# Scan denominators, attention tiles, state residues, loads and an opening run of dense work, in a two-batch hybrid encoder layer

## The chip, the core and the metric

The kernel runs on one core of a Trainium2 chip. The metric is the device time of one execution in microseconds (us). The engines follow their own instruction streams: PE multiplies matrices, ACT (ScalarE), DVE (VectorE) and POOL (GpSimd) work element by element, and SP does nothing here but issue DMA transfers. An engine takes its instructions in order, and an instruction waits where what it needs isn't there, with all that is queued behind it on that engine.

## The reference, cut to what matters

One layer is applied to two batches with the same weights: A, the prompt (1024 tokens), and B, the sample (512 tokens).

```
h = rms_norm(x, pre_w);  cols = h @ w_in          # q|k, v, o, z, gates; attention q,k,v and z; merge gates
mLSTM, 4 heads x 256, both directions, in chunks of 128 tokens:
  sc  = (q k^T) * exp(d_log - mt)
  num = sc v + wa * (q C);   den = sum(sc) + wa * (q n)
  h   = num / max(|den|, exp(-mt))
  C   = decay * C + (k * ws)^T v                  # carried from chunk to chunk
  y_m = o * headnorm(h_fwd + h_bwd) * silu(z)
attention, 3 dilations x 8 heads x 64: logits, row max, exp, product with v, and per head
  y_a = (dilations weighted by their softmax denominators) * silu(z)
merged = sig(g0) * (y_m @ w_pm) + sig(g1) * (y_a @ w_pa)
y = x + rms_norm(merged @ w_out, post_w)
```

All is fp32. The kernel makes a fp32 product out of three matmuls of rounded halves (`mm3`, L194 to L196: high by high, high by low, low by high), so that every weight and activation first gets a high part (ACT, a copy) and a low part (the original less the high part, on DVE or POOL).

## The kernel before

**Two parts.** Up to 1056 us the wide input projections are made, by code that the change does not touch. From 1056 us on PE carries two kinds of work at once: the scans and attentions, whose steps depend on each other through ACT, DVE and POOL, and *dense* units (more columns of the input projection, then `w_pm`, `w_pa`, `w_out`), which depend only on their weights. The dense work is dealt out between the dependent steps so that PE has something to do while the other engines work. The stages, with the dense steps that `STEPS` gives them, are: the scan of A (210 steps, 1056 to 1345 us), the attention of A (202, to 1640 us), the scan of B with the combination of A's dilations beside it (164, to 1835 us), the attention of B (290, to 2100 us), and the combination of B and the last units (86 and what is left, to the end).

**Dense steps and weight tiles.** A dense step is three 128x512 matmuls. Eight steps use one weight tile of 128x1024: SP loads it into one of two buffers `wraw` (L210), ACT makes the high part `wh` (L252), DVE the low part `wl` (L253). There are three pairs of `wh` and `wl` in the scan of A. A `wraw` buffer is loaded anew only after its `wl` is made. `fill.stage(steps, shares)` sets the rate: in the scan of A there are `lead + 74 - 4` shares, `lead` of which are spent at once, ahead of the first product `a` of the scan; with `lead` 4 the rate is 210/74 = 2.84 steps a share and 11 steps go ahead.

**The scan of A** (`mlstm`) has 64 rounds: 4 heads, 8 chunks, 2 directions. `front(k)` makes the weights of a round: POOL masks a row of logarithms (`rm`, L924), ACT takes the exponential (L926), DVE multiplies (L927), ACT rounds (`sch`, L930), POOL takes the rest (`scl`, L931). `core(k)` multiplies: `num` (three or nine matmuls into a PSUM buffer, of which there are two), `kv` (the state's update). Then DVE updates the state `cf` (L977 or L980), ACT copies its high part `ch` (L983), DVE takes its low part `cl` (L984). The denominator follows: DVE takes the maximum (L987) and the reciprocal (L988). In the first half of a head's chunks ACT writes the quotient into `hacc` (L990; the profile calls its buffer X), in the second half DVE adds it there (L993). Only then is the PSUM buffer of `num` free for the round two later, so that PE's `num` waits for L990 or L993.

**The scan of B** (`mlstm_short`) has the same chain of maximum, reciprocal and quotient, at L1186 to L1191.

**The attentions** (`attend`, `att_round`) put a tile through four stages in successive rounds: products `lg` (PE, L1387), softmax (L1399 to L1404), transposes and eviction (`pt` L1410, `pts` L1413), and the product with v (`o` L1422, evicted to `ot` at L1424). There are 12 units u of 8 tiles (A) or 4 tiles (B). The loads of unit u+1 are put in a list when the second tile of unit u begins, and `spread(rounds)` deals them out to SP over so many rounds; the attention of B deals 12 loads over 3 rounds.

**The combination** (`combine`) loads three tiles for each block of 128 tokens (`og`), weighs and adds them. The load for block t+1 is issued when block t begins.

**What sets the order.** The orders of PE and SP are those of the code. For DVE, ACT and POOL a scheduler orders the instructions by priority (the place in the code, unless something is put ahead) and by its own estimate of when they can run. `tc.high_priority()` gives what stands in it a higher priority; `tc.issue_after(x)` keeps what stands in it behind instruction x.

Of the kernel before, what the change touches and what calls it, by code (L numbers as in the profile page):

```python
# [22 lines left out]
F32 = mybir.dt.float32  # L23
# [152 lines left out]
class Net:  # L176
# [680 lines left out]
    def mlstm(self, T, fill, steps, first, banks, lead, after, beside=()):  # L857
# [10 lines left out]
        with ExitStack() as stack:  # L868
# [80 lines left out]
            def core(k):  # L949
                h, i, d = rounds[k]  # L950
                x, m = head[h], made.pop(k)
                c = i if d == 0 else n - 1 - i
                cs = slice(c * P, (c + 1) * P)
                rw = m["rw"]
                v = (x["v"][0][:, c], x["v"][1][:, c])
                if i == d == 0:
                    self.need(("v", h))
                C = x["C"]
                pn = psum("num")
                self.mm3(pn[:, :258], m["sc"], v, True, i == 0)  # L960
                fill(1 / 3)
                if i < n - 1:
                    kh, kl = m["k"]
                    pc = psum("kv")
                    for ct in range(2):
                        self.mm3(pc[:, ct, :258], (kh[:, ct], kl[:, ct]), v, True, True)
                    fill(1 / 3)
                if i > 0:
                    qh, ql = m["q"]
                    _, ch, cl = C[d]  # L970
                    for ct in range(2):
                        self.mm3(pn[:, :258], (qh[:, ct], ql[:, ct]), (ch[:, ct], cl[:, ct]), False, ct == 1)
                if i < n - 1:
                    e = P - 1 if d == 0 else 0
                    if i == 0:
                        cf = sb.tile([P, 2, 258], F32, name=f"cf{d}", bufs=1)
                        nc.vector.tensor_copy(cf, pc[:, :, :258])  # L977
                    else:
                        cf = C[d][0]
                        nc.vector.scalar_tensor_tensor(cf, cf, rw[:, 1, e:e + 1], pc[:, :, :258], op0=OP.mult, op1=OP.add)  # L980
                    ch = sb.tile([P, 2, 258], F32R, name=f"ch{d}", bufs=1)
                    cl = sb.tile([P, 2, 258], F32R, name=f"cl{d}", bufs=1)
                    nc.scalar.activation(ch, cf, AF.Copy)  # L983
                    nc.vector.tensor_sub(cl, cf, ch.bitcast(F32))  # L984
                    C[d] = (cf, ch, cl)
                r = sb.tile([P, 4], F32, name="r", bufs=4)
                nc.vector.tensor_scalar(r[:, 1:2], pn[:, 256:257], m["fl"], pn[:, 257:258], op0=OP.max, op1=OP.max)  # L987
                nc.vector.reciprocal(r[:, 2:3], r[:, 1:2])  # L988
                if i < n // 2:
                    nc.scalar.activation(hacc[:, c], pn[:, :256], AF.Copy, scale=r[:, 2:3])  # L990
                    return
                hs = hacc[:, c]
                nc.vector.scalar_tensor_tensor(hs, pn[:, :256], r[:, 2:3], hs, op0=OP.mult, op1=OP.add)  # L993
                hn = hn_of()
                nc.scalar.activation(hn, hs, AF.Square, accum_out=r[:, 0:1])
                nc.gpsimd.tensor_scalar(r[:, 1:2], r[:, 0:1], 16.0 / 256, 16 * EPS, op0=OP.mult, op1=OP.add)
                nc.gpsimd.tensor_tensor(r[:, 3:4], r[:, 1:2], self.mhalf, op=OP.pow)
                nc.scalar.activation(hn, hs, AF.Copy, scale=r[:, 3:4])

                def turn():  # L1000
                    self.need(("G", h))
                    ph = psum("a")
                    ym = ym_of()
                    for ct in range(2):
                        nc.tensor.transpose(ph[:, ct], hn[:, ct * P:(ct + 1) * P], self.ident)
                    y = ym.rearrange("p (c s) -> p c s", c=2)
                    nc.vector.tensor_mul(y, ph[:, :2], G[:, :, cs])
                    self.put(("ym", S, h), T.ym[2 * h:2 * h + 2, :, cs].rearrange("c p s -> p c s"), y, ym)
                turns[k] = turn
# [94 lines left out]
    def mlstm_short(self, T, fill, steps, first, banks, lead, after, beside=()):  # L1104
# [11 lines left out]
        with ExitStack() as stack:  # L1116
# [56 lines left out]
            def core(k, d):  # L1173
                h, i = rounds[k]
                self.need(("v", h))
                sch, scl = made[k]
                v = head[h]["v"]
                js = list(range(i + 1) if d == 0 else range(i, n))
                pn = psum("num")
                for j in js:  # L1180
                    self.mm3(pn[:, :258], (sch[:, j + d], scl[:, j + d]), (v[0][:, j], v[1][:, j]), j == js[0], j == js[-1])
                if d == 0:
                    sums[k] = sb.tile([P, 8], F32, name="r", bufs=3), sb.tile([P, 256], F32, name="hs")
                r, hs = sums[k]
                o = 64 + 32 * d + h
                nc.vector.tensor_scalar(r[:, d:d + 1], pn[:, 256:257], T.col[:, i, o:o + 1], pn[:, 257:258], op0=OP.max, op1=OP.max)  # L1186
                nc.vector.reciprocal(r[:, 2 + d:3 + d], r[:, d:d + 1])
                if d == 0:
                    nc.scalar.activation(hs, pn[:, :256], AF.Copy, scale=r[:, 2:3])
                    return  # L1190
                nc.vector.scalar_tensor_tensor(hs, pn[:, :256], r[:, 3:4], hs, op0=OP.mult, op1=OP.add)  # L1191
                hn = hn_of()
                nc.scalar.activation(hn, hs, AF.Square, accum_out=r[:, 4:5])
                nc.gpsimd.tensor_scalar(r[:, 5:6], r[:, 4:5], 16.0 / 256, 16 * EPS, op0=OP.mult, op1=OP.add)
                nc.gpsimd.tensor_tensor(r[:, 6:7], r[:, 5:6], self.mhalf, op=OP.pow)
                nc.scalar.activation(hn, hs, AF.Copy, scale=r[:, 6:7])

                def turn():
                    self.need(("G", h))
                    ph = psum("a")  # L1200
                    ym = ym_of()
                    for ct in range(2):
                        nc.tensor.transpose(ph[:, ct], hn[:, ct * P:(ct + 1) * P], self.ident)
                    y = ym.rearrange("p (c s) -> p c s", c=2)
                    nc.vector.tensor_mul(y, ph[:, :2], G[h % 2][:, :, i * P:(i + 1) * P])
                    self.put(("ym", S, h), T.ym[2 * h:2 * h + 2, :, i * P:(i + 1) * P].rearrange("c p s -> p c s"), y, ym)
                turns[k] = turn
# [224 lines left out]
    def attend(self, T, fill, steps, first, banks, outs, after=None, beside=None, at=()):  # L1432
# [5 lines left out]
        with ExitStack() as st:  # L1438
# [26 lines left out]
            for i in range(12):  # L1465
                now = coming
                for j, t in enumerate(now):
                    if j == 1:
                        if i < 11:
                            coming = ready(i + 1)  # L1470
                            self.spread(T.n - 1)
                        elif after:
                            after()
                            self.spread(T.n + 1)
                    self.tick()
                    if j == 0:
                        self.need(("att", i))
                    if j == 1:
                        self.need(("table", i))
                        self.later.pop(i, lambda: None)()  # L1480
                    tiles.append(t)
                    self.att_round(tiles, fill)
                    if len(tiles) in at:
                        next(beside, None)
# [9 lines left out]
    def att_round(self, tiles, fill):  # L1494

        for age, stage in ((0, 0), (1, 1), (2, 2), (None, None), (3, 3)):
            if age is None:
                fill(1)
            elif age < len(tiles) and tiles[-1 - age] is not None:
                tiles[-1 - age][stage]()  # L1500


    def combine(self, T, bank, cs, ys, sb, azs, slow):
# [52 lines left out]
            self.put(("ym", T.S, 4), T.ym[8:12, :, t * P:(t + 1) * P].rearrange("c p s -> p c s"), ya, az)  # L1556

        load(0)
        yield
        az, w = {}, []  # L1560
        for t in range(T.n):
            az[t] = az_of()
            self.fetch(("az", T.S), az[t].rearrange("p (c s) -> p c s", c=4), T.az[:, :, t * P:(t + 1) * P].rearrange("c p s -> p c s"))
            if t + 1 < T.n:
                load(t + 1)
            for step in (lambda: w.append(weigh(t)), lambda: mix(t, w[t]), lambda: add(t)):
                with self.tc.issue_after(self.splits[0].ins), self.tc.issue_after(self.splits[1].ins):
                    step()
                if slow:
                    yield  # L1570
            if not slow:
                yield
                yield
            if t > 0:
                turn(t - 1, az[t - 1])
# [182 lines left out]
def body(tc, a):  # L1758
# [3 lines left out]
    with ExitStack() as st:  # L1762
# [192 lines left out]
        with ExitStack() as s1:  # L1955
# [36 lines left out]
            with ExitStack() as s2:  # L1992
# [2 lines left out]
                sraw = sp.tile([P, BLK + 2], F32R, name="sraw")  # L1995
                N.sg, N.sraw = Rot(N, [sraw[:, :BLK]]), sraw.bitcast(F32)
                head = N.ml_load(A, 0)
                N.mlstm(A, fill, STEPS[0], head, ("a", "num", "kv"), 4,
                        hold("qkv", lambda: N.att_first(A)))
                with ExitStack() as s3:  # L2000
                    lanes = N.lanes_short(B, N.pool(s3, "lane2", 1, "right"), lambda: N.bank("o").rearrange("p a b -> p (a b)"))
# [96 lines left out]
```

## Time and profile before

| quantity | value |
|---|---|
| times of three executions | 2277.72, 2278.14, 2280.95 us (median 2278.14) |
| the profiled execution | 2278.09 us, of which the profile's span is 2276.3 us |
| busy over the span | DVE 64%, ACT 48%, POOL 27% |
| granted clock of PE, mean | 0.995 of full speed |
| DMA | 425 MB, 187 GB/s over the span |

The page of the profile names the costliest groups of instructions, the view of waits tells for each engine what it waited for, the view of windows gives busy time, granted clock of PE and the busy share of the 16 DMA engines for a stretch of time, and the timeline shows single instructions with the idle time ahead of them in brackets. All times of instructions are from the span's start. A DMA that SP issues stands under `SPq`; a group of transfers on one line of a timeline is marked x2 or x3.

### The profile page before, as it was taken

How to read it: one execution, taken by the hardware profiler on the slowest of the kernel's cores; microseconds unless marked ns; L12 is line 12 of the kernel's file. 1: busy time of each engine (PE TensorE's matmuls, PEld its weight loads, DVE VectorE, ACT ScalarE, POOL GpSimd, SP SyncE). 2: the span in 40 equal slices, each digit the busy share in tenths (PEclk: the TensorE clock that was granted, in tenths of full speed). 3: DMA queues.
4: the chain of work that ended last, by engine and by line, in shares of the span. 5: the costliest groups of instructions: out<-in, count | busy, mean ns of one | idle time of the engine just before them, and what ended most of it. 6: DMA issues, size and time to landing. Idle time of an engine off the chain costs nothing. (4 is left out here: it accounts for less than half of the span.)

```text
span 2276.3 us, 35152 instructions
## 1 busy us (share of the span) xinstructions
PE 2235.5 (98%) x12210; PEld 1951.7 (86%) x12210; DVE 1467.8 (64%) x2777; ACT 1100.5 (48%) x2255; POOL 623.6 (27%) x801
## 2 busy tenths in 40 slices
PE   9999999999999999999999999999999999999998
PEld 9999998888887888887888889989888878888787
DVE  5587556767899655643787776675477744556563
ACT  7444223434444433334677766676644354544332
POOL 1000023333333322222567640001033321311311
PEclk9999999999999999999999999999999999999999
DMA  9556435555332223424666559988788888787673
GB/s 355 192 138 143 117 113 194 196 193 195 118 111 101 95 82 109 146 97 159 242 214 218 157 164 250 237 234 216 203 240 264 250 259 221 192 261 208 219 248 116
DMA packets 253627, 425.05 MB, mean 187 GB/s; under 512 B 26209, under 2 KB 150753, under 8 KB 252681
## 3 DMA queue, kind: packets, MB, share of 16 engines
q1 hardware_dynamic: 249848, 410.20, 58.7%
q10 hardware_dynamic: 3600, 12.59, 1.4%
q8 instruction: 97, 1.59, 0.3%
q14 instruction: 82, 0.66, 0.1%
HBM read 302.72 MB, written 128.37 MB: 189 GB/s over the span
## 5 line engine op out<-in xcount | busy, mean ns | idle before, releaser
L194 PE MATMUL dense<-H,wh 128*128 128x512 f32 x672 | 280.5, 417 | 0.0
L196 PE MATMUL dense<-H,wl 128*128 128x512 f32 x672 | 265.6, 395 | 0.5 <-DVE wl L253 0.5
L195 PE MATMUL dense<-H,wh 128*128 128x512 f32 x672 | 264.5, 394 | 0.0
L196 PE MATMUL d<-Hh,phla 128*128 128x512 f32 x608 | 237.4, 390 | 2.2 <-DVE phla L538 2.2
L194 PE MATMUL d<-Hh,phla 128*128 128x512 f32 x608 | 236.9, 390 | 0.0
L195 PE MATMUL d<-Hl,phla 128*128 128x512 f32 x608 | 236.8, 390 | 0.0
L195 PE MATMUL d<-vlo,Hh 128*128 128x322 f32 x704 | 220.4, 313 | 0.8 <-DVE vlo L384 0.8
L196 PE MATMUL d<-vhi,Hl 128*128 128x322 f32 x704 | 220.3, 313 | 0.0
L194 PE MATMUL d<-vhi,Hh 128*128 128x322 f32 x704 | 220.3, 313 | 0.0
L253 DVE TENSOR_TENSOR wl<-wraw,wh 128x1024 fp32r<-128x1024 f32 x109 | 137.0, 1257 | 89.8 <-ACT wh L252 87.7
L556 POOL TENSOR_TENSOR psum_w<-pw_raw 128x512 f32<-128x512 f32 x38 | 57.5, 1512 | 445.8 <-DMA pw_raw<-w_in 422.1
L1399 DVE CUSTOM_DVE_ANT_0 ls<-lg,bias 128x256 f32<-128x256 f32 (+1 forms) x288 | 93.7, 362 | 132.7 <-PE lg L1387 68.2
L194 PE MATMUL d<-Hh,phlb 128*128 128x512 f32 x456 | 177.6, 390 | 0.0
L196 PE MATMUL d<-Hh,phlb 128*128 128x512 f32 x456 | 177.6, 389 | 0.0
L195 PE MATMUL d<-Hl,phlb 128*128 128x512 f32 x456 | 177.6, 389 | 0.0
L1403 ACT ACTIVATE ls<-ls,nm 128x256 f32<-128x256 f32 (+1 forms) x288 | 129.9, 453 | 79.6 <-DVE nm L1401 63.1
L252 ACT ACTIVATE wh<-wraw 128x1024 fp32r<-128x1024 f32 x110 | 116.0, 1054 | 85.1 <-DMA wraw<-w_pm 32.8
L196 PEld LDWEIGHTS dense<-H,wl 128*128 128x128 f32 x672 | 126.7, 189 | 29.7 <-DVE wl L253 0.9
L195 PEld LDWEIGHTS dense<-H,wh 128*128 128x128 f32 x672 | 127.8, 190 | 13.6
L194 PEld LDWEIGHTS dense<-H,wh 128*128 128x128 f32 x672 | 127.4, 190 | 13.5
L196 PEld LDWEIGHTS d<-Hh,phla 128*128 128x128 f32 x608 | 114.1, 188 | 27.6 <-DVE phla L538 4.2
L195 PEld LDWEIGHTS d<-vlo,Hh 128*128 128x128 f32 x704 | 133.5, 190 | 1.5 <-DVE vlo L384 1.4
(556 smaller groups left out, 5722.2 us busy)
## 6 DMA issues: line engine op xcount, KB each, us to landing
pw_raw<-w_in SPq DMA_DIRECT2D x76, 512.0 KB
wraw<-w_in SPq DMA_DIRECT2D x76, 512.0 KB
aqk_a<-pwk SPq DMA_DIRECT2D x48, 512.0 KB
aqk_b<-sw SPq DMA_DIRECT2D x48, 256.0 KB
wraw<-w_pm SPq DMA_DIRECT2D x24, 512.0 KB
wraw<-w_out SPq DMA_DIRECT2D x24, 512.0 KB
vb<-w_vp SPq DMA_DIRECT2D x16, 644.0 KB
va<-w_vp SPq DMA_DIRECT2D x14, 644.0 KB
```

What stands on the lines that cost most here:

```text
L194: nc.tensor.matmul(out, lh, rh, start=start, stop=False)
L195: nc.tensor.matmul(out, lh, rl, start=False, stop=False)
L196: nc.tensor.matmul(out, ll, rh, start=False, stop=stop)
L252: self.splits = (nc.scalar.activation(hi[:, :n], raw[:, :n], AF.Copy), on.tensor_sub(lo[:, :n], raw[:, :n], hi[:, :n].bitcast(F32)))
L253: on.tensor_sub(lo[:, :n], raw[:, :n], hi[:, :n].bitcast(F32)))
L556: self.nc.gpsimd.tensor_add(s[:, 0], ws[1][:, 0], ws[1][:, 1])
L1399: nc.vector.tensor_tensor_reduce(out=ls[:, hh], in0=ts["lg"][hh], in1=bt[:, hh], scale=1.0, scalar=NEG, op0=OP.add, op1=OP.max, accum_out= ...
L1403: nc.scalar.activation(ls[:, hh], ls[:, hh], AF.Exp, bias=nm[:, hh:hh + 1], accum_out=ot[:, 128 + hh:129 + hh])
```

## The change

- In both scans the chain of maximum, reciprocal and quotient is put in high priority, and in the scan of A the low part `cl` of the state is moved in the code behind that chain, to be issued after its last DVE instruction.
- In both attentions all four stages of a tile are put in high priority.
- In the attention of B the loads of unit 1 are dealt out in one round instead of three.
- The combination loads two blocks at the start, and block t+2 once block t is used.
- The scan of A takes `lead` 8 instead of 4: 78 shares, 210/78 = 2.69 steps a share, and 22 steps ahead of the first product instead of 11.

```
                 nc.scalar.activation(ch, cf, AF.Copy)
-                nc.vector.tensor_sub(cl, cf, ch.bitcast(F32))
                 C[d] = (cf, ch, cl)
             r = sb.tile([P, 4], F32, name="r", bufs=4)
-            nc.vector.tensor_scalar(r[:, 1:2], pn[:, 256:257], m["fl"], pn[:, 257:258], op0=OP.max, op1=OP.max)
-            nc.vector.reciprocal(r[:, 2:3], r[:, 1:2])
+            hs = hacc[:, c]
+            with self.tc.high_priority():
+                nc.vector.tensor_scalar(r[:, 1:2], pn[:, 256:257], m["fl"], pn[:, 257:258], op0=OP.max, op1=OP.max)
+                last = nc.vector.reciprocal(r[:, 2:3], r[:, 1:2])
+                if i < n // 2:
+                    nc.scalar.activation(hs, pn[:, :256], AF.Copy, scale=r[:, 2:3])
+                else:
+                    last = nc.vector.scalar_tensor_tensor(hs, pn[:, :256], r[:, 2:3], hs, op0=OP.mult, op1=OP.add)
+            if i < n - 1:
+                with self.tc.issue_after(last.ins):
+                    nc.vector.tensor_sub(cl, cf, ch.bitcast(F32))
             if i < n // 2:
-                nc.scalar.activation(hacc[:, c], pn[:, :256], AF.Copy, scale=r[:, 2:3])
                 return
-            hs = hacc[:, c]
-            nc.vector.scalar_tensor_tensor(hs, pn[:, :256], r[:, 2:3], hs, op0=OP.mult, op1=OP.add)
...
-                            self.spread(T.n - 1)
+                            self.spread(T.n - 1 if i or T.n > 4 else 1)
...
             elif age < len(tiles) and tiles[-1 - age] is not None:
-                tiles[-1 - age][stage]()
+                with self.tc.high_priority():
+                    tiles[-1 - age][stage]()
...
         load(0)
+        load(1)
         yield
...
-            if t + 1 < T.n:
-                load(t + 1)
-            for step in (lambda: w.append(weigh(t)), lambda: mix(t, w[t]), lambda: add(t)):
+            for i, step in enumerate((lambda: w.append(weigh(t)), lambda: mix(t, w[t]), lambda: add(t))):
                 with self.tc.issue_after(self.splits[0].ins), self.tc.issue_after(self.splits[1].ins):
                     step()
                 if slow:
                     yield
+                    if i == 1 and t + 2 < T.n:
+                        load(t + 2)
             if not slow:
                 yield
+                if t + 2 < T.n:
+                    load(t + 2)
                 yield
...
-                N.mlstm(A, fill, STEPS[0], head, ("a", "num", "kv"), 4,
+                N.mlstm(A, fill, STEPS[0], head, ("a", "num", "kv"), 8,
```

Three places show how instructions stand before and now.

**ACT at the start of the scan of A** (from 1071 us). Here `sw` is the eviction of a dense result, `wh_8712` the high part of the third weight tile, `wh_8708` and `wh_8710` of the fourth and fifth, `st` and `K` evictions of the first head's preparation, `sch` the first round's weights. Before:

```order
L894 ACTIVATE st_8794<-a 128x512
L930 ACTIVATE sch<-rm 128x128
L902 ACTIVATE K_8779<-a 128x2x256
L945 ACTIVATE kh<-K_8779,col_382 128x256
L902 ACTIVATE K_8779<-a 128x2x256
L926 ACTIVATE rm<-rm,col_382 128x128
L894 ACTIVATE st_8794<-a 128x512
L252 ACTIVATE wh_8712<-wraw_8706 128x1024
```

Now, in the same place:

```order
L641 ACTIVATE sw_8775<-dense 128x512
L252 ACTIVATE wh_8712<-wraw_8706 128x1024
L252 ACTIVATE wh_8708<-wraw_8707 128x1024
L252 ACTIVATE wh_8710<-wraw_8706 128x1024
L894 ACTIVATE st_8794<-a 128x512
L902 ACTIVATE K_8779<-a 128x2x256
L930 ACTIVATE sch<-rm 128x128
```

Three weight tiles, from the third on, have moved ahead of the first eviction `st` of the scan.

**DVE at the last head's first two rounds** (L987 and L988 before are L988 and L989 now; L984 is L996). `wl_8709` is the low part of a weight tile, `cf` the state's first copy, `cl` its low part, `ym` and `kl` belong to other rounds. Before:

```order
L987 TENSOR_SCALAR r<-num,col_382 128x1
L927 TENSOR_TENSOR rm<-rm,st_8795 128x128
L988 RECIPROCAL r<-r 128x1
L977 COPY cf_11942<-kv 128x516
L946 SCALAR_TENSOR_TENSOR kl<-K_11028,col_382,kh 128x256
L1007 TENSOR_TENSOR ym_8805<-a,X_8807 128x256
L984 TENSOR_TENSOR cl_11945<-cf_11942,ch_11944 128x516
L987 TENSOR_SCALAR r<-num,col_382 128x1
L988 RECIPROCAL r<-r 128x1
L977 COPY cf_12002<-kv 128x516
L253 TENSOR_TENSOR wl_8709<-wraw_8707,wh_8708 128x1024
```

Now:

```order
L988 TENSOR_SCALAR r<-num,col_382 128x1
L989 RECIPROCAL r<-r 128x1
L253 TENSOR_TENSOR wl_8709<-wraw_8707,wh_8708 128x1024
L977 COPY cf_11955<-kv 128x516
L1012 TENSOR_TENSOR ym_8805<-a,X_8807 128x256
L988 TENSOR_SCALAR r<-num,col_382 128x1
L946 SCALAR_TENSOR_TENSOR kl<-K_11049,col_382,kh 128x256
L989 RECIPROCAL r<-r 128x1
L996 TENSOR_TENSOR cl_11958<-cf_11955,ch_11957 128x516
L927 TENSOR_TENSOR rm<-rm,st_8795 128x128
L977 COPY cf_12012<-kv 128x516
```

The low part of the weight tile has moved a round ahead, and `cl` stands behind the second round's chain.

**SP at the start of the attention of B** (from 1835 us). `Q` and `V1a` are the loads of unit 1 (their x counts transfers on one row), `bias` a table, `w_pm` weights, `ymr` and `sraw` rows of the scan's output that are split for `w_pm`. Before:

```order
L231 DMA Q_18005<-aqk_b 64x512 x2
L231 DMA V1a<-aqk_b 64x512 x3
L210 DMA wraw_8706<-w_pm 128x1024
L231 DMA ymr_18368<-ym_a 128x512
L210 DMA wraw_8707<-w_pm 128x1024
L231 DMA ymr_18369<-ym_a 128x512
L231 DMA V1a<-aqk_b 64x512
L231 DMA Q_18005<-aqk_b 64x512 x2
L231 DMA V1a<-aqk_b 64x512 x2
...
L231 DMA sraw<-ym_a 128x512
L231 DMA V1a<-aqk_b 64x512 x2
L231 DMA bias_8768<-erep 128x256 x2
```

Now:

```order
L231 DMA Q_18008<-aqk_b 64x512 x2
L231 DMA V1a<-aqk_b 64x512 x4
L231 DMA Q_18008<-aqk_b 64x512 x2
L231 DMA V1a<-aqk_b 64x512 x4
L231 DMA bias_8768<-erep 128x256 x2
L210 DMA wraw_8706<-w_pm 128x1024
L231 DMA ymr_18368<-ym_a 128x512
L210 DMA wraw_8707<-w_pm 128x1024
L231 DMA ymr_18369<-ym_a 128x512
```

All loads of unit 1 have moved ahead of the weights of `w_pm` and the rows that go with them.

More of the change, by code (lines that the diff above doesn't have):

```diff
@@ L1185, in core @@
                 o = 64 + 32 * d + h
[L1186 to L1191, printed above, removed]
+                with self.tc.high_priority():
+                    nc.vector.tensor_scalar(r[:, d:d + 1], pn[:, 256:257], T.col[:, i, o:o + 1], pn[:, 257:258], op0=OP.max,
+                                            op1=OP.max)
+                    nc.vector.reciprocal(r[:, 2 + d:3 + d], r[:, d:d + 1])
+                    if d == 0:
+                        nc.scalar.activation(hs, pn[:, :256], AF.Copy, scale=r[:, 2:3])
+                        return
+                    nc.vector.scalar_tensor_tensor(hs, pn[:, :256], r[:, 3:4], hs, op0=OP.mult, op1=OP.add)
                 hn = hn_of()
@@ L1499, in att_round @@
             elif age < len(tiles) and tiles[-1 - age] is not None:
-                tiles[-1 - age][stage]()
+                with self.tc.high_priority():
+                    tiles[-1 - age][stage]()
     def combine(self, T, bank, cs, ys, sb, azs, slow):
```

## The prediction

> **What bounds the kernel now.** I read the page first, then what PE waited for, then the windows around each wait.
>
> ```profile
> PE 2235.5 (98%) x12210; PEld 1951.7 (86%) x12210; DVE 1467.8 (64%) x2777; ACT 1100.5 (48%) x2255; POOL 623.6 (27%) x801
> ...
> PE num L194 <- ACT X L990: 6.8, 6, 2.3
> PE lg L1387 <- DMA sraw<-ym_a: 4.7, 1, 4.7
> PE a L892 <- DMA K<-qk_a: 3.7, 2, 2.3
> PE num L194 <- ACT rm L926: 1.3, 1, 1.3
> PE num L194 <- DVE X L993: 0.9, 2, 0.5
> ...
> PE pt L1410 <- ACT ls L1403: 2.5, 3, 1.0
> ...
> PE num L196 <- POOL scl L1170: 1.1, 1, 1.1
> ```
>
> PE is busy for 98% of the span, and the change takes no matmul away: it can win only in the waits of PE (a row gives the total in us, how often, and the longest), and in what follows a wait. The quotient copy L990 holds `num` six times, 6.8 us in all; unit 1 of B's attention costs one wait of 4.7 us. What follows a wait is seen in the windows, whose last three columns are PE's granted clock, the DMA share and GB/s:
>
> ```profile
> 1056.00:1084.00 28.00, 23.78 (x124) 19.93 (x124) 11.33 (x20) 13.11 (x25) 6.76 (x19) 0.94 0.81 285
> 1084.00:1100.00 16.00, 12.73 (x74) 10.65 (x73) 11.62 (x24) 9.82 (x25) 8.23 (x13) 0.98 0.98 355
> 1100.00:1101.00 1.00, 1.00 (x6) 0.90 (x5) 0.23 (x1) 0.61 (x2) 0.36 (x2) 0.50 1.04 385
> 1292.00:1294.00 2.00, 2.00 (x8) 1.71 (x8) 1.36 (x4) 0.80 (x2) 0.63 (x2) 0.50 1.05 240
> 1860.00:1900.00 40.00, 39.65 (x218) 34.45 (x219) 16.67 (x46) 19.66 (x48) 12.56 (x14) 0.95 1.01 282
> ```
>
> Behind each wait of 2.26 us or more the clock falls to half for some 3 us (two rows at 0.50 show the middle of it). In the first row that is 28 x 0.06 = 1.7 us lost while PE counts as busy; in the last, 40 x 0.05 = 2.0 us. I add 1.7 us to each such wait, and 2.0 us to that of 4.7 us.
>
> **Lead 8, the start of the scan of A.** Rows of PE, ACT, DVE and SP:
>
> ```profile
> 1056.51 0.39 PE L194 MATMUL dense<-H,wh 128*128 128x512 f32 x1
> ...
> 1063.76 0.39 PE L196 MATMUL dense<-H,wl 128*128 128x512 f32 x1
> 1065.62 0.49 PE L892 MATMUL a<-Q,K 128*128 128x128 f32 x2 [1.47 <-DMA K<-qk_a]
> 1068.37 1.91 PE L892 MATMUL a<-Q,K 128*128 128x128 f32 x9 [2.26 <-DMA K<-qk_a]
> 1079.75 0.50 PE L196 MATMUL dense<-H,wl 128*128 128x512 f32 x1 [0.49 <-DVE wl L253]
> ...
> 1077.38 1.06 ACT L252 ACTIVATE wh<-wraw 128x1024 fp32r<-128x1024 f32 x1 [0.22 <-DMA wraw<-w_in]
> 1078.47 1.22 DVE L253 TENSOR_TENSOR wl<-wraw,wh 128x1024 fp32r<-128x1024 f32 x1 [0.99 <-ACT wh L252]
> ...
> 1068.71 11.34 SPq L210 DMA_DIRECT2D wraw<-w_in  x3
> ```
>
> Eleven steps (33 matmuls) take from 1056.51 to 1063.76, so 0.68 us a step. Before, PE then lost 1.47 + 2.26 + 0.5 us in waits and 1.7 us by the clock: 5.9 us. Now 22 steps stand ahead, but two weight tiles carry only 16, which end at 1056.5 + 16 x 0.68 = 1067.4. The third tile's load keeps its place on SP behind Q, K and V (1068.71, landed by 1077.4), so `wh` is ready at 1077.38 + 1.06 = 1078.4 and `wl` at 1079.7, with the DMA and not the order of ACT as the cause. PE waits 11.0 us, then 0.4 us for `wl`, and the clock costs 1.7 us: 13.1 us. The loads of Q and K are there by then. **Difference +7.2 us.** It is not all kept: the first head's later waits come from loads that do not wait for PE.
>
> ```profile
> 1091.13 0.39 PE L194 MATMUL num<-V0a,sch 128*128 128x258 f32 x1 [0.68 <-ACT X L990]
> 1092.78 0.39 PE L194 MATMUL kv<-V0a,kh 128*128 128x258 f32 x1 [0.30 <-DVE cf L980]
> 1098.19 0.39 PE L194 MATMUL num<-V0a,sch 128*128 128x258 f32 x1 [2.29 <-ACT X L990]
> ...
> 1096.55 0.40 ACT L926 ACTIVATE rm<-rm,col 128x128 f32<-128x128 f32 x1 [1.05 <-POOL rm L924]
> ...
> 1097.69 0.45 ACT L990 ACTIVATE X<-num,r 128x256 f32<-128x256 f32 x1
> ```
>
> The copy L990 at 1097.69 stood on ACT behind the exponential L926, which waited for POOL's mask of a row from DRAM, in a stretch with a DMA share of 0.98. With PE some 7 us later the rows are there first: 0.68 + 0.30 + 2.29 and 1.7 us of clock go, -5.0 us. Bounds of the pair: +7.2 (nothing paid back) to +0.5 (the clock drop overlaps); I take **+2.2 us**.
>
> A rule of the Trainium skill bears on the clock (TensorE: Matmul & The Clock Gate, Part 1): the clock is halved after at least one idle window of about 3.4 us. By it the waits of 2.3 us need cost no clock; the rows at 1100 and 1292, each behind a wait of 2.3 us, show that they do here, so the sum goes by the rows.
>
> **The rounds of the scan of A.**
>
> ```profile
> 1148.01 0.36 PE L194 MATMUL num<-V0a,sch 128*128 128x258 f32 x1 [1.25 <-ACT rm L926]
> 1157.93 0.39 PE L194 MATMUL num<-V1a,sch 128*128 128x258 f32 x1 [0.93 <-ACT X L990]
> 1289.74 0.39 PE L194 MATMUL num<-V1a,sch 128*128 128x258 f32 x1 [2.32 <-ACT X L990]
> ...
> 1288.43 0.40 ACT L926 ACTIVATE rm<-rm,col 128x128 f32<-128x128 f32 x1 [1.98 <-POOL rm L924]
> ...
> 1287.07 1.33 POOL L924 TENSOR_SCALAR_AFFINE_SELECT rm<-rw 128x128 f32<-128x128 f32 x1
> ...
> 1289.30 0.28 POOL L924 TENSOR_SCALAR_AFFINE_SELECT rm<-rw 128x128 f32<-128x128 f32 x1
> ...
> 1287.04 1.22 DVE L253 TENSOR_TENSOR wl<-wraw,wh 128x1024 fp32r<-128x1024 f32 x1
> ```
>
> The denominator's DVE steps are rarely what is late: at 1289.74 the copy waited behind an exponential that waited for POOL's mask, and the mask took 1.33 us beside a low part on DVE, against 0.28 us two masks later. High priority does not move the copy ahead of that exponential (the order of ACT keeps it there). But the low part `wl` moves a round ahead on DVE, so I let the mask run without it: about 1 us less wait. I count -0.8 and, with 1.5 us left, no clock drop: -2.5 us. For the waits on L993 (0.9 us), whose addition now follows its reciprocal directly, -0.9. At 1148.01 half of the 1.25, -0.6 (0 to 1.25). Against it: at 1157.93 a weight tile's `wh` (1.06 us) and a result's eviction now stand between exponential and copy, 0 to 1.6 us, I take +0.8; and each round has 0.15 of a step (0.10 us) less dense work to cover it, which counts in the nine rounds that wait: +0.9. Sum **-2.3 us**. Bounds: all waits of the later heads and the clock go, 6.8 - 3.0 + 1.3 + 0.9 + 1.7 = 7.7 us gained; nothing gained and both costs, 1.7 us lost. The value is near the lower gain, since ACT's order hardly changes. `cl` moves behind the chain: it is used two rounds later, and I cost it at nothing; if that cover is gone, PE waits for it in `num` of each round.
>
> **The loads of unit 1 in B's attention.**
>
> ```profile
> 1837.27 1.23 SPq L231 DMA_DIRECT2D Q<-aqk_b  x2
> 1838.60 2.09 SPq L231 DMA_DIRECT2D V1a<-aqk_b  x3
> 1841.65 0.34 SPq L210 DMA_DIRECT2D wraw<-w_pm  x1
> ...
> 1854.11 1.09 SPq L231 DMA_DIRECT2D V1a<-aqk_b  x2
> ...
> 1855.11 0.48 PE L1387 MATMUL lg<-V1a,Q 128*128 128x256 f32 x2
> 1860.34 1.15 PE L1387 MATMUL lg<-V1a,Q 128*128 128x256 f32 x2 [4.74 <-DMA sraw<-ym_a]
> ...
> 1870.36 0.40 PE L194 MATMUL dense<-V0b,wh 128*128 128x512 f32 x1
> ```
>
> The row of waits names `sraw`; what PE waited for is the last pair of `V1a`, issued behind it at 1854.11 and used at 1860.34, some 6 us later. Issued in a row, twelve loads at 0.6 to 0.7 us each end at 1837.3 + 12 x 0.7 = 1845.7, or 1847 with small waits for a free slot; 6 us to land gives 1853, ahead of the need at 1855.1. So 4.7 + 2.0 us go. What is late next: the `w_pm` loads, from 1841.65 to about 1847, and the rows of `ymr` behind them. Products with `w_pm` began at 1870.36 and now begin about 7 us earlier, while DMA is full until 1900 (share 1.01): the bytes are the same, so part of the wait may come back at the rows `ymr` or at unit 2. I give back 2 us: **-4.7 us** (bounds: -6.7, and +1 if the relay costs more).
>
> **The rest.** Priority in A's attention: its longest row of waits is 2.5 us on an exponential, and ACT's order there is nearly the old one: 0 (-1.5 to +1.5). The scan of B waits 1.1 us for POOL, which the change leaves; the `og` loads come a block earlier: -0.5 (+-1). Other stages: 0.
>
> **Sum**: 2278.09 (the profiled execution, beside a median of 2278.14) + 2.2 - 2.3 - 4.7 - 0.5 = **2272.8 us**. A measurement of this kernel tells about 0.2% from no change, 4.6 us: faster means under 2273.6, slower over 2282.7.
>
> **The rivals.**
> 1. *Priority does more.* All later waits on L990, L926 and L993 go: -7.7 in place of -2.3, 2267.4 us. For it, three of those waits name ACT; against it, they are ACT's waits for POOL. Chance 0.15.
> 2. *The rounds do not change.* The change doesn't do what it says, since the copy stays where it was on ACT: 0 in place of -2.3, 2275.1 us, the same. Chance 0.14.
> 3. *The wait at unit 1 is relayed* to unit 2 or to the `w_pm` rows, as DMA is full: 2277.5 us. For it the share of 1.01 up to 1900, against it that products with `w_pm` begin only at 1870. Chance 0.11.
> 4. *The lead is not paid back*: the rows of the first head move back with PE, because SP takes its turns from the code; +5.0, 2277.8 us. Chance 0.07.
> 5. *Slower: the dense work starves in A's attention.* Tile stages put ahead delay `wh` and `wl` on ACT and DVE, and PE waits for a low part at each tile. The one such wait in the trace is 0.5 us; 202 steps are 25 tiles, 12.6 us: 2285.4 us. It decides once 20 of the 25 tiles are late. For it, ACT makes the exponentials, evictions and high parts one after the other; against it, its order is nearly the old one. Chance 0.09.
> 6. *Waits of 2.3 us do not decide the clock*: then two times 1.7 us less is won (first and last head), 2276.2 us. The two rows at 0.50 speak against it. It is what the Trainium skill's rule would give (same page and part). Chance 0.04.
>
> My forecast has the remaining 0.40, from 2270 to 2275.5 us: 0.29 of it faster, 0.11 the same. Faster: 0.29 + 0.15 = 0.44. Slower: rival 5 with 0.02 each of rivals 3 and 4, 0.13. The same: the rest, 0.43. The range reaches from rival 1 with some more of the unknown gain, 2264.5, to above rivals 3 and 4 with 1 to 4 us of their own costs, 2281.5; rival 5 and the outer ends are left out.
>
> **What would show it.** PE's wait before the 17th dense step should be near 11 us and end about 1078.4, with a half clock behind it; no wait on `K` at all; the first head's wait of 2.29 us gone; the mask beside 1289 well under 1 us; no wait over 1 us at `lg` of unit 1, and the last `V1a` issued before 1848. I am wrong if the third tile is loaded sooner, if the waits on L990 stay (2 or more of over 2 us), or if DMA stays full and a wait of 3 us or more stands between 1860 and 1900.

## The result, and the profile after

| kernel | executions | median us | range us |
|---|---|---|---|
| before | 10 | 2278.94 | 2273.20 to 2280.95 |
| changed | 10 | 2288.42 | 2283.12 to 2298.03 |

The ratio is 1.0042 (95% interval 1.0028 to 1.0057): the change costs 6 to 13 us. The forecast was 2272.8 us, 5.3 us faster, so the sign was wrong. The profile of the changed kernel is of its slowest execution (2298.03 us), 9.6 us over its median; what is read from it below is held against the profiles of the experiments. One execution of the experiment e9 took 3143 us at a granted clock of 0.654 and is left out of its figures.

What PE waited for in the changed kernel (us in total, times, longest):

```profile
PE dense L194 <- ACT wh L252: 11.5, 1, 11.5
PE o L1429 <- ACT ot L1431: 7.6, 5, 3.1
PE dense L194 <- DVE H L1663: 3.1, 1, 3.1
PE kv L194 <- DVE cf L980: 3.0, 3, 1.7
PE num L194 <- DVE X L993: 2.7, 1, 2.7
...
PE num L194 <- ACT X L991: 1.8, 2, 1.3
```

The waits that the prediction spoke of are gone or small: the quotient copy (L990, now L991) from 6.8 to 1.8 us, no row for K, no wait for unit 1's loads at `lg` (4.7 us before). New rows stand in their place: 11.5 us for the third weight tile, 7.6 us of `o` for `ot`, 3.1 us for `H`, and 2.7 and 3.0 us in the scan for DVE.

The start of the scan of A, on PE, ACT and SP:

```profile
1066.79 0.39 PE L196 MATMUL dense<-H,wl 128*128 128x512 f32 x1
1078.69 0.80 PE L194 MATMUL dense<-H,wh 128*128 128x512 f32 x1 [11.52 <-ACT wh L252]
...
1077.58 1.06 ACT L252 ACTIVATE wh<-wraw 128x1024 fp32r<-128x1024 f32 x1 [5.23 <-DMA wraw<-w_in]
...
1068.55 11.70 SPq L210 DMA_DIRECT2D wraw<-w_in  x3
```

PE had done its 16 steps at 1067.2, and the 17th began at 1078.69, when the third tile's high part was ready; its load was issued at 1068.55, as before. This is the wait of 11.0 us that was forecast to end at 1078.4. The windows behind it show the clock:

```profile
1056.00:1084.00 28.00, 16.45 (x62) 12.63 (x61) 8.22 (x11) 7.09 (x12) 3.79 (x14) 0.76 0.78 274
...
1080.00:1082.00 2.00, 2.00 (x5) 1.61 (x6) 1.15 (x1) 0.00 (x0) 0.00 (x0) 0.50 0.40 84
```

PE is busy for 16.45 us of the 28 (23.78 before), and behind the wait it runs at half clock.

To see where time goes over the whole, I take the length of each stage from its first to the next stage's first matmul (start: first dense step to the first `num`; scan A: to the first `lg`; attention A: to the next `num`; scan B: to the next `lg`; attention B: to the last `o`; end: to the last matmul). The kernels e2 to e14 are those of the experiments.

| stage, us | before | changed | e2 lead 8 | e6 combine | e5 | e9 | e10 | e14 |
|---|---|---|---|---|---|---|---|---|
| start | 24.3 | 38.9 | 38.0 | 25.1 | 24.7 | 37.9 | 26.8 | 21.9 |
| scan A | 271.1 | 262.1 | 262.3 | 269.2 | 264.3 | 261.3 | 262.7 | 264.5 |
| attention A | 313.7 | 316.5 | 314.6 | 316.3 | 314.2 | 316.5 | 316.3 | 313.4 |
| scan B | 169.0 | 169.4 | 169.3 | 169.0 | 169.0 | 169.5 | 169.1 | 169.5 |
| attention B | 286.8 | 291.4 | 290.5 | 289.8 | 285.6 | 285.4 | 285.8 | 285.3 |
| end | 148.2 | 155.1 | 145.9 | 155.1 | 147.1 | 146.7 | 146.7 | 146.4 |

With lead 8 the start holds 10 dense steps (6.8 us) more, which the scan then has less. So the start costs 14.6 - 6.8 = 7.8 us (forecast 7.2), and the scan of A wins 9.0 - 6.8 = 2.2 us (forecast 5.0 + 2.3). Even these 2.2 us are not clear of chance: four other profiles with the scan's code as before (e4, e6, e12, e13) give it 267.3 to 269.2 us, and 262.1 + 6.8 = 268.9 lies among them. The end is 7 us longer, where nothing was forecast.

### The profile page after: what moved, and what is told of

It is laid out like the page before. It is cut to its first block, busy times and chain, and to the rows that moved or that the text cites. A ratio compares the mean times of both kernels' runs of the same rounds, so it can differ in the third digit from the quotient of the medians.

```text
span 2296.2 us, 35148 instructions
## 1 busy us (share of the span) xinstructions
PE 2240.2 (98%) x12210; PEld 1954.8 (85%) x12210; DVE 1470.4 (64%) x2777; ACT 1101.2 (48%) x2255; POOL 617.2 (27%) x801
## 5 line engine op out<-in xcount | busy, mean ns | idle before, releaser
L194 PE MATMUL dense<-H,wh 128*128 128x512 f32 x672 | 281.4, 419 | 11.5 <-ACT wh L252 11.5
```

The source lines that it names most:

```text
L194: nc.tensor.matmul(out, lh, rh, start=start, stop=False)
```

## The experiments

Each was timed in five rounds against the kernel before; a ratio stands with its 95% interval, and a difference in us is the ratio's distance from 1 times 2277. Diffs are against the kernel that the text names.

**e1. The change with lead 4.**

```
-                N.mlstm(A, fill, STEPS[0], head, ("a", "num", "kv"), 8,
+                N.mlstm(A, fill, STEPS[0], head, ("a", "num", "kv"), 4,
```

> The change with lead 4 in place of 8. Theory (the lead's wait of 11.5 us for the third weight tile is not paid back: the first two stages end 5.2 us later in the profile of the changed kernel): about 5 us less than the changed kernel, so +4 to +5 us over before, near 2283, and PE's wait for the third tile back under 1 us, the waits on K back at 3.7 us. Rival (the lead costs nothing in the end, the loss stands in the attentions and the last stage): no difference from the changed kernel, near 2288.

Measured 2277.19 us, ratio 0.9999 (0.9989 to 1.0008). Without the lead the rest of the change is worth nothing in sum. The lead costs more than the theory's 5 us; but the end of this kernel takes 158.2 us, so gains elsewhere are hidden by a loss there.

**e2. The kernel before with lead 8.** The reverse of that edit, on the kernel before.

> The kernel before with lead 8 and nothing else. Theory: +5 us, near 2284, with the wait of about 11 us ahead of the 17th dense step and the scan of A ending some 5 us later. Rival (the scan's waits are what they are because of the denominator's part, and the lead is paid back): within 1.5 us of before.

Measured 2284.15 us, ratio 1.0030 (1.0016 to 1.0044), +6.8 us: the theory. The wait is there (11.12 us at 1077.99), and the first head's later waits are gone but for 0.2 us.

**e3. The change without the attention's priority.**

```
             elif age < len(tiles) and tiles[-1 - age] is not None:
-                with self.tc.high_priority():
-                    tiles[-1 - age][stage]()
+                tiles[-1 - age][stage]()
```

> The change without the high priority on the attention's stages. Theory (with priority the eviction of o stands on ACT behind splits that wait for rows from DRAM, and PE waits for it in B's attention, 7.6 us in the profile): 5 to 8 us less than the changed kernel, 2280 to 2283, and the row of o waiting for ot back to about 1 us. Rival (the loads dealt out in one round and the og loads issued early make DMA late, whatever ACT's order is): no difference, near 2288, with the waits on ot or on the rows still there.

Measured 2286.49 us, ratio 1.0045 (1.0028 to 1.0062), as the whole change. The theory fell: the waits of `o` for `ot` are there without the priority, too, as PE's waits in this kernel show.

```profile
PE dense L194 <- ACT wh L252: 10.8, 1, 10.8
PE o L1429 <- ACT ot L1431: 4.6, 4, 2.0
PE dense L194 <- DVE H L1662: 3.7, 1, 3.7
```

This also says that the 3.1 us for `H` is no accident of the slow execution.

**e4. The kernel before with unit 1's loads in one round.**

```
-                            self.spread(T.n - 1)
+                            self.spread(T.n - 1 if i or T.n > 4 else 1)
```

> The kernel before with the loads of unit 1 in B's attention dealt out in one round, and nothing else. Theory: the wait of 4.7 us at lg of unit 1 goes with its 2 us of clock, and little comes back: -4 to -6 us, near 2274. Rival (the relay: DMA is full, the wait moves to the rows for w_pm or to unit 2): within 1.5 us of before, with a wait of 3 us or more between 1860 and 1900.

Measured 2274.44 us, ratio 0.9990 (0.9979 to 1.0001), -2.3 us: between the two, with an interval that reaches into both. The wait of 4.7 us is gone, but `o` now waits 4.9 us for `ot`, where it waited 1.1 us before (1.7 to 2.7 us in e2, e6 to e8, e12 and e13, which deal the loads out as before). PE's row in the view of waits:

```profile
PE o L1422 <- ACT ot L1424: 4.9, 6, 1.3
```

and ACT's timeline ahead of that eviction at one of the six places:

```profile
1863.62 1.06 ACT L252 ACTIVATE X<-wraw 128x1024 fp32r<-128x1024 f32 x1 [0.84 <-DMA wraw<-w_pm]
1864.59 1.13 ACT L1603 ACTIVATE K<-ymr 128x512 fp32r<-128x512 f32 x2
1865.63 0.26 ACT L1424 ACTIVATE ot<-o 128x128 f32<-128x128 f32 x1
```

The eviction stands on ACT behind a weight tile that waited for its DMA and behind two splits. There is one PSUM buffer for `o` in B's attention, so PE waits. The relay is on ACT, through loads that now come later.

**e5. The change with lead 4 and the combination's loads as before.** Left are the denominator, the priorities and unit 1's loads. Beside the edit of e1, the loads of the combination go back:

```
         load(0)
-        load(1)
         yield
...
+            if t + 1 < T.n:
+                load(t + 1)
...
-                    if i == 1 and t + 2 < T.n:
-                        load(t + 2)
...
-                if t + 2 < T.n:
-                    load(t + 2)
```

> The change with lead 4 and with the combination's loads as before; left of it are the denominator's part, the priority of the attention and the loads of unit 1 in one round. Theory (the loads of block t+2 make SP wait for DVE, some 7 us in the profile of the change with lead 4, and what is queued behind them on SP comes late: the last stage takes 154 to 158 us instead of 148): 6 to 9 us less than the change with lead 4, so near 2269, last stage at 146 to 149 us. Rival (the last stage is late because the attention of B ends earlier and weights are always as late as DMA lets them): near 2277, last stage still over 153 us.

Measured 2270.39 us, ratio 0.9971 (0.9958 to 0.9984), -6.6 us, the end at 147.1 us: the theory. The combination's loads were what hid the gain in e1.

**e6. The kernel before with the combination's loads of the change.** The reverse of the edit of e5, on the kernel before.

> The kernel before with the combination's loads of the change, and nothing else. Theory: +5 to +9 us, near 2284, last stage at 153 us or more, PE waiting over 2 us for a gate (gab) behind it. Rival: within 1.5 us of before.

Measured 2286.81 us, ratio 1.0036 (1.0023 to 1.0050), +8.2 us, the end at 155.1 us and 3.9 us of waiting for `H`. SP's waits in the last stage, of this kernel:

```profile
SPq L231 <- DVE X L1541: 7.3, 1, 7.3
```

and of the kernel before:

```profile
SPq L231 <- DVE X L1541: 0.6, 2, 0.4
```

L231 is the load of `og` and L1541 (L1549 in the change) DVE's reading of the block that the load overwrites. In the kernel before that block had been read long ago. SP's timeline in e6 around it:

```profile
2141.43 0.90 SPq L1748 DMA_DIRECT2D xo<-x_prompt  x2
2149.65 1.56 SPq L231 DMA_DIRECT2D V0a<-og_b  x3
...
2162.52 1.26 SPq L210 DMA_DIRECT2D wraw<-w_pm  x2
...
2170.95 0.34 SPq L210 DMA_DIRECT2D wraw<-w_pm  x1
2171.35 0.90 SPq L231 DMA_DIRECT2D gab<-gt_b  x2
```

For 7 us SP issues nothing (2142.3 to 2149.65), and what is queued behind comes late: weights of `w_pm`, and the gate `gab` without which DVE can't write `H`. DVE and PE then wait:

```profile
2175.40 0.69 DVE L1655 SCALAR_TENSOR_TENSOR H<-gab,dense 128x512 f32<-128x512 f32 x1 [3.19 <-DMA gab<-gt_b]
...
2176.24 0.76 PE L194 MATMUL dense<-V0b,wh 128*128 128x512 f32 x1 [3.88 <-DVE H L1655]
```

From 2100 us on PE waits 9.2 us in all here, and 3.9 us in the kernel before.

**e7. The kernel before with the scan's denominator part** (the high priority and `cl` behind it, as in the first part of the change's diff).

> The kernel before with the scan of A's denominator chain in high priority and cl behind it, and nothing else. Theory: the scan of A ends 3 to 6 us earlier (the change with lead 4 ends it 264 us after the first product num, before took 267 to 271 us), so 2271 to 2274. Rival (that difference is only how the first head's wait falls from execution to execution): within 1.5 us of before.

Measured 2274.20 us, ratio 0.9988 (0.9977 to 0.9998), -2.7 us. Its waits in the scan of A:

```profile
PE num L194 <- ACT X L991: 4.7, 3, 2.3
PE a L892 <- DMA K<-qk_a: 4.0, 2, 2.1
PE num L194 <- DVE X L993: 0.5, 1, 0.5
```

Six waits for the copy (6.8 us) have become three (4.7 us): the one at 1098 in the first head (2.29 us) and two of 0.3 us in the third are gone. The wait for the exponential at 1148 (1.25 us) is gone, too. The wait of 2.3 us at the last head, on which the forecast put its gain, is still there.

**e8. The kernel before with thinner cover.**

```
-STEPS = (210, 202, 164, 290, 86)
+STEPS = (199, 213, 164, 290, 86)
```

> The kernel before with 199 dense steps in the scan of A and 213 in the attention of A (210 and 202 before); lead 4 and 11 steps ahead as before, but 2.69 steps a share, as with lead 8. Theory (the rounds of the scan wait for ACT, DVE and POOL, and dense work is what hides it: 0.15 step or 0.10 us less in each of 64 rounds comes back as waiting): the waits of the scan behind the first head grow by 4 to 6 us, time +4 to +6 us, near 2282. Rival (with lead 8 those waits grew because the weight tiles fell on other rounds): within 2 us of before.

Measured 2277.05 us, ratio 1.0000 (0.9989 to 1.0011). The theory fell: a twentieth less dense work in each round costs nothing that shows (the interval is 2.5 us either way). The wait of 2.7 to 3.0 us that the kernels with lead 8 have at the start of the second head is 0.3 us here, so it isn't due to the thinner cover. For their lesser waits this isn't settled, since e8 has some of its own (1.95 us at the third head, 1.1 us at the end of the scan).

**e9. The change with the combination's loads as before** (lead 8; the edit of e5 without the lead).

> The whole change (lead 8) but for the combination's loads. The parts so far: lead 8 alone +7, the combination's loads alone +9, denominator -3, the loads of unit 1 -2.5, all but lead and combination -6.5. Theory (the parts add up): about +0.5 to +2 over before, near 2279, 8 us less than the whole change. Rival (the lead's cost and the combination's have a cause in common, DMA being late): 2271 or 2286.

Measured 2281.62 us, ratio 1.0018 (1.0008 to 1.0029), +4.1 us, above the theory's sum. Against e5 the lead costs 0.0047, or 10.7 us, where alone it cost 6.8 us. The intervals of the two overlap, so the times alone don't show that the parts fail to add up.

**e10. As e9, the third weight tile's load issued first.**

```
+                N.flush(lambda p: p[1][0] == "w")
                 head = N.ml_load(A, 0)
```

> As the run before, but SP issues the load of the third weight tile ahead of Q, K and V of the first head; the same 22 steps ahead and the same 2.69 steps a share. Theory (the wait for that tile, 11 us and a half clock, is what the lead costs): the wait is gone and those on K too, the scan of A ends 8 us or more sooner than with lead 8, 2266 to 2271. Rival (with 22 steps ahead and thinner rounds the scan waits more later on, whatever the start): 2275 or more, the waits at the first to second head (2.7 us with lead 8) and at the end (1.6 us) being still there.

Measured 2269.36 us, ratio 0.9969 (0.9957 to 0.9981): 11 us less than e9, with the same steps ahead and the same rate. So the wait for the third tile is what the lead costs. SP's timeline:

```profile
1042.37 8.11 SPq L210 DMA_DIRECT2D wraw<-w_in  x3
1059.42 0.80 SPq L231 DMA_DIRECT2D Q<-qk_a  x2
```

All three tiles go out before Q. The rival's waits are nevertheless there: PE waits 2.9 us for L993, of which 2.73 us stand at 1148.20, and 1.7 us at the end of the scan. So they don't come from the long wait, and with them e10 is no better than e5.

**e11. The change with lead 5 and the combination's loads as before.**

> The change without the combination's loads and with lead 5: 14 steps ahead, which need only the two weight tiles that are there. Theory: no wait for the third tile, the waits on K shorter by about 2 us and no half clock there: 0 to 4 us less than with lead 4, 2267 to 2270. Rival (any dense step taken out of the rounds costs what it gains): 2270 to 2273.

Measured 2275.57 us, ratio 0.9997 (0.9987 to 1.0006), 6 us more than with lead 4: both theories fell. The tile is again the cause, as PE's timeline shows:

```profile
1077.41 0.79 PE L194 MATMUL dense<-H,wh 128*128 128x512 f32 x1 [5.65 <-ACT wh L252]
```

Fourteen steps ahead leave two steps for the work between the first products, and PE stands at the 17th step here as well. This profile is of an execution of 2281.73 us, 6 us over the median; that the tile is the cause is shown by e14.

**e12. The kernel before with the attention's priority** (the reverse of the edit of e3).

> The kernel before with the high priority of the attention's stages, and nothing else. Theory (from the sums of the other parts): between -2 and +2 us, the attention of A within 1.5 us of before (313.7 us from its first lg to the next scan's first num). Rival (the priority puts the eviction of o behind splits that wait for DRAM, and PE waits for it): +3 us or more, with waits of o on ot over 4 us in sum.

Measured 2276.68 us, ratio 0.9996 (0.9987 to 1.0006), the attention of A 313.2 us: no difference, as the theory had it.

**e13. The kernel before with the combination's first two loads at the start**, and the later ones where they were.

```
         load(0)
+        load(1)
         yield
...
-            if t + 1 < T.n:
+            if 0 < t < T.n - 1:
                 load(t + 1)
```

> The kernel before, in which only the load of block 1 in the combination moves to the start; the load of block t+1 stays at the start of block t from t = 1 on, so that SP never waits at it for the block in work. Theory (SP stands at the load of block t+2 until DVE has read its buffer, and weights and gates behind it come late): within 2 us of before, last stage 148 us. Rival (the early load itself takes DMA time from weights): +5 us or more, last stage 153 us or more.

Measured 2277.16 us, ratio 1.0004 (0.9995 to 1.0013), the end at 146.2 us: the theory. In its last stage the same row of SP's waits reads

```profile
SPq L231 <- DVE X L1541: 1.4, 2, 1.2
```

The early load of block 1 is free. What costs is the place at which the later loads are issued, where SP stands and waits.

**e14. As e11 (lead 5), the third tile's load first** (the edit of e10).

> The change without the combination's loads, lead 5, third weight tile issued ahead of Q, K and V. Theory (the third tile's arrival is what dense work ahead runs into, also at lead 5, where its wait was 5.7 us): 5 us or more less than lead 5 without it, 2267 to 2271. Rival (lead 5 is slow because of where its weight tiles fall among the rounds): 2274 or more.

Measured 2264.65 us (2263.51 to 2269.08), ratio 0.9954 (0.9942 to 0.9966): 10 us faster than before, and the best of all kernels here. The start takes 21.9 us, though it holds three steps more than e5's, with one wait on K of 2.0 us in place of two and no wait for a tile. More than half of the gain may be clock: the mean granted clock of its executions is 0.998, that of the kernel before beside them 0.9955, which over 2265 us makes some 6 us (an estimate, and a high one, as a half clock costs nothing while PE waits). The head of PE's waits:

```profile
PE o L1429 <- ACT ot L1431: 5.2, 7, 1.1
PE kv L194 <- DVE cf L980: 2.7, 3, 1.7
PE pt L1417 <- ACT ls L1410: 2.3, 3, 0.9
PE a L892 <- DMA K<-qk_a: 2.0, 1, 2.0
```

**e15. The same with lead 4.**

> As the run before with lead 4. Theory: the waits on K grow by about 1.4 us, as 512 KB go ahead of them, and the 0.5 us at the third tile goes: within 2 us of the change with lead 4 and the combination's loads as before, 2270. Rival (the place of the tile is worth something at any lead): 2268 or less.

Measured 2271.25 us, ratio 0.9982 (0.9969 to 0.9996), as e5. With 11 steps ahead the tile's place is worth nothing that shows; there has to be dense work that uses it.

## Why the prediction was wrong, step by step

| part | forecast us | alone, us (interval) | from |
|---|---|---|---|
| lead 8 | +2.2 | +6.8 (3.6 to 10.0) | e2 |
| denominator in the scan of A | -2.3 | -2.7 (-5.2 to -0.5) | e7 |
| unit 1's loads in one round | -4.7 | -2.3 (-4.8 to +0.2) | e4 |
| attention's priority | 0 | -0.9 (-3.0 to +1.4) | e12 |
| combination's loads, the rest | -0.5 | +8.2 (5.2 to 11.4) | e6 |
| sum | -5.3 | +9.1; the whole change +9.6 (6.4 to 13.0) | |

**The step that failed in kind is "The rest": "the `og` loads come a block earlier: -0.5 (+-1). Other stages: 0."** Of the 14.9 us between forecast and measurement, 8.7 belong to this part, 4.6 to the lead and 2.4 to unit 1's loads. The step looked at when the data come, not at what SP does meanwhile. The change moves the load of block t+2 to the place where block t has only just been handed to DVE, so SP, which takes its instructions in order, waits there for DVE's reading, 7.2 us in e1, 7.3 in e6 (0.6 before), and in the changed kernel

```profile
SPq L231 <- DVE X L1549: 8.2, 1, 8.2
```

and weights and gates queue behind it. The prediction counted such moves for the attention of B and not here. e6 shows the price, and e13 that the waiting place is the cause: the early load of block 1 kept, the place of the others put back, and the cost is gone. The same row of the table of parts also holds the high priority in the scan of B, which was not tried alone; that stage takes 169.0 us before and 169.0 to 169.5 us in every kernel that has it, which leaves it nothing to explain.

**The lead: the mechanism was right and the first size, too; the payback was not.** PE's wait was forecast at 11.0 us and measured 10.8 to 11.5 us in four profiles, and e10 shows it to be the cause. "0.68 + 0.30 + 2.29 and 1.7 us of clock go, -5.0 us" failed in three ways. The waits of the first head did go (0.2 to 0.3 us are left in e2, e3 and e9), but their price came from one execution: in four other profiles of the same code (e4, e6, e12, e13) the wait of 2.29 us is 1.1 to 1.9 us, and no half clock stands behind it. Secondly the denominator part takes the same wait away (e7 has none at 1098), so it can be won only once; the measured cost of the lead, 10.7 us beside that part and 6.8 us alone, goes that way, though the intervals overlap. Thirdly waits came that were not there before: with lead 8 PE waits 2.7 to 3.0 us at the start of the second head, 1.3 to 1.5 us at the third and 1.7 us at the end of the scan. The timelines of DVE and PE at the first of these, in the changed kernel:

```profile
1151.98 1.23 DVE L253 TENSOR_TENSOR wl<-wraw,wh 128x1024 fp32r<-128x1024 f32 x1
1153.13 0.68 DVE L642 SCALAR_TENSOR_TENSOR sw<-dense,sw 128x512 fp32r<-128x512 f32 x1
1153.73 0.47 DVE L946 SCALAR_TENSOR_TENSOR kl<-K,col,kh 128x256 fp32r<-128x256 f32 x1
1154.13 0.27 DVE L988 TENSOR_SCALAR r<-num,col 128x1 f32<-128x1 f32 x1
...
1156.18 0.55 PE L194 MATMUL num<-V0a,sch 128*128 128x258 f32 x1 [2.73 <-DVE X L993]
```

DVE reaches the maximum L988 there only behind a tile's low part, a dense result's sum and `kl`, high priority or not. That the tile falls on this round because of the 11 steps more is likely: e8, with the same rate and 11 steps ahead, has 0.3 us at this place, e10, without the long wait, 2.7 us, and e11, with 14 steps ahead, 2.1 us. Which of the three instructions decides was not tried and stays open. The rival that the lead isn't paid back had a chance of 0.07 and another reason; what was missing is a rival in which the lead and the denominator win the same waits.

**The denominator: the size was right, the place was not.** The forecast put 2.5 of its us on the last head's wait. With lead 4 this wait stays at 2.3 us (e1, e5, e7), so there the sum came out right through other waits, those at 1098 and 1148, and the match is partly luck. In the changed kernel the wait is 0.55 us, as forecast, with the masks ahead of it at 0.3 to 0.7 us (1.33 us before), and it is as short in e3, e9 and e10; with lead 8 alone (e2) it is 1.9 us. So it takes the lead as well, and the scan with lead 8 is no shorter for it (see the stages). That the copy would stand further back at 1157.93 held: 0.93 us became 1.53 us in e7.

**Unit 1's loads: the mechanism was right, the relay probably larger than counted.** The wait at `lg` went in every kernel with this part (without it, it is 3.7 to 7.3 us from profile to profile). Of the 6.7 us some 4.4 came back, not 2, though the interval of e4 just reaches the forecast: `o` waits for `ot`, 4.9 us in e4 against 1.1 to 2.7 us in the kernels without this part. The prediction looked for the relay at unit 2 and at the rows; at the place shown in e4 it stood on ACT, where rows and weights that wait for DMA hold up an eviction.

**The attention's priority** did nothing that shows (-3.0 to +1.4 us), as forecast, and the forecast's rival for the slower side (low parts late in A's attention) didn't occur; the slower side came from a place that had been costed at nothing.

## What to carry to other kernels

A load moved in the code moves a wait, too: ask of each moved load which engine still reads its buffer at the new place, and what stands behind it on the queue that issues it. Work put ahead of a stage as cover helps only as far as its own inputs are there; here 22 steps with the third weight tile late cost 6.8 us, while 14 steps with that tile loaded first, the best of the combinations tried, took 6 us off the same kernel with 11 steps (e14 against e15). Two parts of a change that remove the same wait are not to be added without a look at what each leaves, and the price of a wait wants more than one execution.

## What was not expected of the hardware

The prediction took it that a wait of 2.26 us or more is followed by a half clock, at 1.7 us each. The same wait of the last head says otherwise. In e5 (wait of 2.30 us at 1284.83) the clock stays at full speed:

```profile
1284.00:1286.00 2.00, 1.17 (x7) 1.04 (x8) 1.18 (x4) 2.00 (x6) 0.67 (x2) 1.00 0.42 141
1286.00:1288.00 2.00, 2.00 (x15) 1.87 (x14) 1.76 (x4) 1.51 (x5) 1.06 (x2) 1.00 0.84 204
```

In e7 (2.30 us at 1283.45) it falls:

```profile
1283.00:1285.00 2.00, 1.55 (x6) 1.34 (x7) 0.98 (x3) 2.00 (x7) 0.30 (x2) 0.77 0.46 155
1285.00:1287.00 2.00, 2.00 (x9) 1.82 (x8) 1.08 (x2) 1.17 (x5) 1.05 (x2) 0.50 1.03 234
```

Of eight profiles with this wait at 2.30 to 2.34 us, the clock fell in five (before, e6, e7, e13, e15) and not in three (e1, e4, e5), and in e8 it fell behind a wait of 1.95 us at the third head. Of the five profiles with a wait of 2.7 to 3.0 us at the start of the second head it fell in three (the changed kernel, e3, e9) and not in two (e2, e10). For waits of 2 to 3 us the length does not decide it. The Trainium skill (TensorE: Matmul & The Clock Gate, Part 1) says that the window in which activity is watched is free-running, so that a wait can fall in different places of it; that the same wait goes either way agrees with this. Its length of about 3.4 us for an idle window does not agree: half clocks stand here behind waits of 1.95 and 2.3 us. The waits of 11 us were followed by a half clock in all four profiles that have them, as the prediction had it.
